# A hybrid SSD, Hyena and PEER block: one-hots of eight tokens in one comparison, 16-bit key lookup, expert activations kept in PSUM

## The chip, the cores and the metric

The kernel runs on one core of a Trainium2 chip. The metric is the time of one execution in microseconds (us) of device time: 4247.77 us before, the median of three runs (4242.83 to 4251.62). Engines: TensorE (PE, with PEld for its weight loads) multiplies matrices, VectorE (DVE), ScalarE (ACT) and GpSimd (POOL) work on elements, SyncE (SP) issues DMAs. SBUF is the on-chip memory, PSUM the small memory into which TensorE writes.

## The reference

One layer of a diffusion backbone over 1024 tokens of width 1024, with a context of 256. Two kinds of token mixing (a bidirectional Mamba-2 scan and a gated long convolution) come first, and the channel mixing after them, PEER, is the part that concerns us. Cut to it:

```python
def block(hb):                                    # 128 tokens
    q = (hb @ wq).reshape(128, 8, 2, 128)
    s = einsum('thsd,snd->thsn', q, subkeys)      # 8 heads, two key sets of 128
    s1, i1 = top_k(s[:, :, 0], 16)
    s2, i2 = top_k(s[:, :, 1], 16)
    sc, ci = top_k(all 256 sums s1 + s2, 16)
    e1 = i1 at ci // 16;  e2 = i2 at ci % 16
    idx = e1 * 128 + e2                           # one of 16384 experts
    gate = softmax(sc)
    act = gelu(hb . u_tab[idx]) * gate            # 8 x 16 experts per token
    return sum of act * v_tab[idx]
```

## The kernel before

Mixing and output projection take the first 1740 us or so and are not touched. Then eight blocks of 128 tokens are treated in two ways. For the last three blocks (`NB - ND`) the rows of the chosen experts are gathered from DRAM, one DMA of 128 rows at a time on GpSimd's queue, and VectorE multiplies them (class `Experts`, `gathered`). For the first five (`ND`, 640 tokens) every one of 128 groups of 128 experts is computed densely on TensorE, and a table of gates, mostly zeros, picks the chosen ones.

Routing. `firsts` multiplies tokens with the keys (`qacc`) and takes the 16 best per half with VectorE's max, index and replace instructions (`top16`); the 32-bit integer indices `r_ix` are cast to `r_idx`. `second` takes the 16 best of 112 candidate sums, splits their positions (`r_pos`, `r_pof`), and looks up the key index by a one-hot `r_oh` of 16 per choice, multiplied by the indices on GpSimd and summed on VectorE. `spread` builds the gate table of a block: for every token a one-hot of the first key times the gate (128 choices in the partitions, 128 keys in the row) and a one-hot of the second key, whose product on TensorE is the token's 128x128 table. It takes eight tokens at a time: the first one-hot (`e1`, named `r_e` in the trace, as is `e2`) of two tokens is made on ScalarE, of two on GpSimd and of four on VectorE, the second ones in one comparison on VectorE. A table goes to DRAM by `r_st`. GpSimd also makes the low parts of the keys (`wk_l`).

All products with 32-bit accuracy are made of a rounded high part and the rest (`split`: ScalarE copies to the high part, VectorE or GpSimd subtracts). `score` multiplies one expert group's `u` (parts `x_uh`, `x_ul`) with the 640 tokens in two halves of 320 (24 matmuls each, PSUM tile `x_s`, two banks) and applies Gelu. 48 groups (`NE`, `AHEAD`) are scored during the routing (`beside`) and stored in DRAM as `d_A`.

Expert stage (`run`). Groups go by four (`SC`). `up` loads or scores a group's activations `x_a`, multiplies them by the gates `x_g` and splits them to `x_ah`, `x_al`. `down` multiplies these with the group's value rows (`x_vh`, `x_vl`, made from `x_vr` by `load_v` on ScalarE and GpSimd) for one block and half of the columns, and VectorE adds the result `x_acc` to `x_o`. Between them `some` calls up the next gathered rows.

The order on each engine is not the order of the code: a scheduler places each instruction by a simulated time line within what data and buffers permit. Each engine works its list in that order; one that waits holds up all behind it on its engine.

Of the kernel before, what the change touches and what calls it, by code (L numbers as in the profile page):

```python
# [10 lines left out]
F32 = mybir.dt.float32  # L11
# [1268 lines left out]
E1A = 2  # L1280
RB = 4
E1P = 2
# [7 lines left out]
class Route:  # L1290
# [70 lines left out]
    def first(self, b, c, terms, wk, ps, bufs):  # L1361
# [9 lines left out]
        ix = wk.tile([128, 2, 16], U32, name="r_ix", bufs=2)  # L1371
        tmp = wk.tile([128, 128], F32, name="r_tmp", bufs=2)
        for j in range(2):
            self.top16(self.val[:, b, 2 * c + j], ix[:, j], sc[:, j], tmp)
        nc.vector.tensor_copy(self.idx[:, b, 2 * c:2 * c + 2], ix)
# [11 lines left out]
    def second(self, b, wk):  # L1387
# [4 lines left out]
        val, idf = self.val[:, b], self.idx[:, b]  # L1392
# [18 lines left out]
        V.tensor_copy(pof, pos)  # L1411
# [7 lines left out]
        for t in range(2):  # L1419
            oh = wk.tile([128, 8, 16, 16], F32, name="r_oh", bufs=1)  # L1420
# [3 lines left out]
            nc.gpsimd.tensor_mul(oh, oh, idf[:, t:16:2, None, :].to_broadcast([128, 8, 16, 16]))  # L1424
            yield
            if t < TRD:
                for n in (8, 4, 2, 1):
                    nc.gpsimd.tensor_add(oh[..., :n] if n > 1 else e[:, t, :, :, None], oh[..., :n], oh[..., n:2 * n])
            else:
                V.tensor_reduce(e[:, t].rearrange("p h k -> p (h k)"), ohv, axis=AX.X, op=ALU.add)  # L1430
# [13 lines left out]
    def spread(self, b, ef, g, wk, ps, pq):  # L1444
# [6 lines left out]
        T = wk.tile([128, 4, 128], F32, name="r_T", bufs=2)  # L1451
        nc.scalar.activation(T[:, :3], p[:, :3], AF.Copy)
        nc.scalar.activation(T[:, 3], p[:, 2], AF.Copy, scale=-1.0)
        for q in range(128 // GT):
            st = wk.tile([128, 128, GT], F32, name="r_st", bufs=2)
            for t8 in range(GT // 8):
                t0 = q * GT + t8 * 8
                e1 = wk.tile([128, 8, 128], F32, name="r_e1", bufs=3)
                for m in range(8):
                    t = t0 + m  # L1460
                    if m < E1A:
                        nc.scalar.activation(e1[:, m], self.iota, AF.Abs, scale=-1.0, bias=T[:, 0, t:t + 1])
                        nc.scalar.activation(e1[:, m], e1[:, m], AF.Relu, scale=T[:, 3, t:t + 1], bias=T[:, 2, t:t + 1])
                    elif m < E1A + E1P:
                        nc.gpsimd.tensor_scalar(e1[:, m], self.iota, T[:, 0, t:t + 1], T[:, 2, t:t + 1],
                                                op0=ALU.is_equal, op1=ALU.mult)
                    else:
                        V.scalar_tensor_tensor(e1[:, m], self.iota, T[:, 0, t:t + 1],
                                               T[:, 2, t:t + 1].to_broadcast([128, 128]), op0=ALU.is_equal, op1=ALU.mult)
                e2 = wk.tile([128, 8, 128], F32, name="r_e2", bufs=2)  # L1470
                (nc.gpsimd if t8 < E2P else V).tensor_tensor(e2, self.iota[:, None, :].to_broadcast([128, 8, 128]),
                                T[:, 1, t0:t0 + 8, None].to_broadcast([128, 8, 128]), op=ALU.is_equal)
# [10 lines left out]
class Experts:  # L1483
# [24 lines left out]
    def beside(self, x, tiles):  # L1508
# [3 lines left out]
        while self.n < min(int(self.ahead), NE):  # L1512
            self.K.nc.sync.dma_start(self.K.T["A"][self.n], self.score())
# [112 lines left out]
    def score(self):  # L1626
# [10 lines left out]
        a = wk.tile([128, TD], F32, name="x_a", bufs=XA)  # L1637
        for m in range(SN):
            ms = slice(m * SW, (m + 1) * SW)
            s = ps.tile([128, 512], F32, name="x_s", bufs=2)  # L1640
# [293 lines left out]
```

## Time and profile before

| | us |
|---|---|
| median of three runs | 4247.77 |
| profiled execution | 4236.63 |
| its span, first to last instruction | 4234.9 |
| busy: PE, DVE | 3766.8, 3434.8 |
| busy: ACT, POOL | 1373.3, 2218.0 |

The mean granted clock of TensorE is 0.947 of full speed. All rows below come from the profiled execution, which is 11 us shorter than the median. Busy time is that in which an engine had an instruction in work, which includes the time that an instruction stood still after it began. Where a group of instructions of one form shows a mean well over its median, some of them stood.

### The profile page before, as it was taken

How to read it: one execution, taken by the hardware profiler on the slowest of the kernel's cores; microseconds unless marked ns; L12 is line 12 of the kernel's file. 1: busy time of each engine (PE TensorE's matmuls, PEld its weight loads, DVE VectorE, ACT ScalarE, POOL GpSimd, SP SyncE). 2: the span in 40 equal slices, each digit the busy share in tenths (PEclk: the TensorE clock that was granted, in tenths of full speed). 3: DMA queues.
4: the chain of work that ended last, by engine and by line, in shares of the span. 5: the costliest groups of instructions: out<-in, count | busy, mean ns of one | idle time of the engine just before them, and what ended most of it. 6: DMA issues, size and time to landing. Idle time of an engine off the chain costs nothing. (4 is left out here: it accounts for less than half of the span.)

```text
span 4234.9 us, 59929 instructions
## 1 busy us (share of the span) xinstructions
PE 3766.8 (89%) x21481; PEld 3307.3 (78%) x21481; DVE 3434.8 (81%) x6389; ACT 1373.3 (32%) x2567; POOL 2218.0 (52%) x1723
## 2 busy tenths in 40 slices
PE   5999999898888887789998877899989999989995
PEld 4787887777877786688998876788878888878884
DVE  5665887556889795599999996798878888878998
ACT  3233333326454121232225665222222222222221
POOL 2232323244344221065737785676767677667675
PEclk9999999998898998899999999999999999999997
DMA  6333433467774546567645546899989999989997
GB/s 209 103 123 103 130 112 133 134 194 223 228 233 142 168 148 180 166 214 250 232 134 206 201 170 218 285 338 322 354 314 340 317 326 340 342 310 341 337 322 258
DMA packets 509674, 974.09 MB, mean 230 GB/s; under 512 B 33771, under 2 KB 291231, under 8 KB 506432
## 3 DMA queue, kind: packets, MB, share of 16 engines
q1 hardware_dynamic: 395616, 557.25, 40.2%
q0 software_dynamic: 110880, 405.98, 26.2%
q10 hardware_dynamic: 2880, 7.03, 0.5%
q8 instruction: 169, 2.77, 0.3%
q14 instruction: 129, 1.06, 0.1%
HBM read 823.20 MB, written 146.95 MB: 229 GB/s over the span
## 5 line engine op out<-in xcount | busy, mean ns | idle before, releaser
L1643 PE MATMUL x_s<-fTh,x_uh 128*128 128x320 f32 x2048 | 640.9, 313 | 12.1 <-ACT x_a L1644 11.9
L1643 PE MATMUL x_s<-fTh,x_ul 128*128 128x320 f32 x2048 | 638.9, 312 | 7.2 <-DVE x_ul L1604 7.2
L1643 PE MATMUL x_s<-fTl,x_uh 128*128 128x320 f32 x2048 | 640.0, 313 | 0.0
L1683 PE MATMUL x_acc<-x_vl,x_ah 128*128 128x512 f32 x1280 | 514.1, 402 | 15.1 <-POOL x_vl L1615 15.1
L1683 PE MATMUL x_acc<-x_vh,x_ah 128*128 128x512 f32 x1280 | 449.8, 404 | 82.7 <-ACT x_vh L1614 60.8
L1520 POOL DMA_INDIRECT rows<-in_peer_u_dram,ids x384 | 415.1, 1081 | 197.3 <-DVE rows L1544 65.1
L1557 DVE SCALAR_TENSOR_TENSOR e_p<-rows,e_a,e_p 128x1024 f32<-128x1024 f32 x381 | 489.8, 1286 | 30.6 <-DMA rows<-in_peer_v_dram,ids 19.2
L1683 PE MATMUL x_acc<-x_vh,x_al 128*128 128x512 f32 x1280 | 509.6, 399 | 0.0
L1544 DVE SCALAR_TENSOR_TENSOR rows<-rows,e_p 128x1024 f32<-128x1024 f32 x384 | 455.5, 1210 | 41.7 <-DMA rows<-in_peer_u_dram,ids 39.6
L1520 POOL DMA_INDIRECT rows<-in_peer_v_dram,ids x384 | 397.7, 1036 | 140.5 <-issue 64.0
L1615 POOL TENSOR_TENSOR x_vl<-x_vr,x_vh 128x512 fp32r<-128x512 f32 x256 | 340.8, 1335 | 190.1 <-ACT x_vh L1614 178.9
L1643 PEld LDWEIGHTS x_s<-fTh,x_uh 128*128 128x128 f32 x2048 | 389.3, 190 | 25.8 <-ACT x_a L1644 16.7
L1643 PEld LDWEIGHTS x_s<-fTh,x_ul 128*128 128x128 f32 x2048 | 389.0, 190 | 17.0 <-DVE x_ul L1604 8.3
L1643 PEld LDWEIGHTS x_s<-fTl,x_uh 128*128 128x128 f32 x2048 | 389.3, 190 | 9.2
L1683 PEld LDWEIGHTS x_acc<-x_vh,x_ah 128*128 128x128 f32 x1280 | 241.9, 193 | 135.5 <-ACT x_vh L1614 67.5
L1683 PEld LDWEIGHTS x_acc<-x_vl,x_ah 128*128 128x128 f32 x1280 | 247.7, 194 | 69.3 <-POOL x_vl L1615 23.5
L1614 ACT ACTIVATE x_vh<-x_vr 128x512 fp32r<-128x512 f32 x256 | 159.7, 627 | 421.8 <-DMA x_vr<-in_peer_v_dram 351.4
L1683 PEld LDWEIGHTS x_acc<-x_vh,x_al 128*128 128x128 f32 x1280 | 247.2, 193 | 48.9
L199 PE MATMUL mm<-xl,whi 128*128 128x512 f32 (+1 forms) x784 | 263.6, 410 | 8.2 <-DVE xl L51 8.2
L199 PE MATMUL mm<-xh,whi 128*128 128x512 f32 (+1 forms) x784 | 263.9, 412 | 7.4 <-DVE acc L235 3.6
L51 POOL TENSOR_TENSOR wlo<-wraw,whi 128x1024 fp32r<-128x1024 f32 (+1 forms) x49 | 121.1, 2473 | 280.9 <-ACT whi L50 260.3
L199 PE MATMUL mm<-xh,wlo 128*128 128x512 f32 (+1 forms) x784 | 263.3, 411 | 0.4 <-POOL wlo L51 0.4
(382 smaller groups left out, 8748.9 us busy)
## 6 DMA issues: line engine op xcount, KB each, us to landing
x_raw<-in_peer_uT_dram SPq DMA_DIRECT2D x128, 512.0 KB
x_vr<-in_peer_v_dram SPq DMA_DIRECT2D x256, 256.0 KB
d_G<-r_st SPq DMA_DIRECT2D x20, 2048.0 KB
x_g<-d_G SPq DMA_DIRECT2D x32, 1280.0 KB
wraw<-in_w_mod_dram SPq DMA_DIRECT2D x32, 1024.0 KB
wraw<-in_w_in_dram SPq DMA_DIRECT2D x24, 1024.0 KB
wk_w<-d_WK SPq DMA_DIRECT2D x24, 1024.0 KB
d_kr<-h_k SPq DMA_DIRECT2D x32, 512.0 KB
```

Source lines behind the costliest of these rows:

```text
L51: (self.nc.gpsimd if pool else self.nc.vector).tensor_sub(lo, src, hi.bitcast(F32))
L199: nc.tensor.matmul(p, w[:, k], x[j][:, k, t0:t0 + n], start=(k == 0 and q == 0), stop=(k == 7 and q == 2))
L1520: nc.gpsimd.indirect_dma_start(out=r, out_offset=None, in_=table, in_offset=bass.IndirectOffsetOnAxis(ap=ids[:, j:j + 1], axis=0))
L1544: nc.vector.scalar_tensor_tensor(r, r, 1.0, f, op0=ALU.mult, op1=ALU.mult, accum_out=d[:, j:j + 1])
L1557: nc.vector.scalar_tensor_tensor(acc, r, a[:, j:j + 1], acc, op0=ALU.mult, op1=ALU.add)
L1614: nc.scalar.activation(hi, raw, AF.Copy)
L1615: self.pace = nc.gpsimd.tensor_sub(lo, raw, hi.bitcast(F32)).ins
L1643: nc.tensor.matmul(s[:, :SW], w[:, k], x[:, k, ms], start=(k == 0 and q == 0), stop=(k == 7 and q == 2))
L1683: self.K.nc.tensor.matmul(p, a[x][:, bs], v[w], start=(m == 0 and q == 0), stop=(m == SC - 1 and q == 2))
```

## The change

Four edits, all after 1740 us.

- `top16` writes its indices straight into `r_idx`, now a 32-bit integer table; `second` casts a block's 256 indices at once to 16 bits (`r_if`) on ScalarE, as it does the positions.
- The key one-hot `r_oh` is made in 16 bits with two buffers; its product with the key indices moves from GpSimd to VectorE.
- In `spread`, one comparison on VectorE makes the first one-hots of eight tokens (`e0`). Three tokens (`GP`) are multiplied by the gate in one instruction on GpSimd, five on ScalarE, one copy each with the gate as scale. The negated gates are no longer needed.
- In the expert stage, Gelu writes back to PSUM; the gate product is made there in halves of 320, and both parts are taken from there. A loaded activation is multiplied from SBUF into a score bank, so that it takes both banks too.

```diff
-        self.idx = mid.tile([128, NB, 16, 16], F32, name="r_idx")
+        self.idx = mid.tile([128, NB, 16, 16], U32, name="r_idx")
...
-        nc.vector.tensor_copy(self.idx[:, b, 2 * c:2 * c + 2], ix)
...
-        val, idf = self.val[:, b], self.idx[:, b]
+        val = self.val[:, b]
+        idf = wk.tile([128, 16, 16], BF16, name="r_if", bufs=1)
+        nc.scalar.activation(idf, self.idx[:, b], AF.Copy)
...
-        V.tensor_copy(pof, pos)
+        nc.scalar.activation(pof, pos, AF.Copy)
...
-            oh = wk.tile([128, 8, 16, 16], F32, name="r_oh", bufs=1)
+            oh = wk.tile([128, 8, 16, 16], BF16, name="r_oh", bufs=2)
...
-            nc.gpsimd.tensor_mul(oh, oh, idf[:, t:16:2, None, :].to_broadcast([128, 8, 16, 16]))
+            V.tensor_mul(oh, oh, idf[:, t:16:2, None, :].to_broadcast([128, 8, 16, 16]))
...
-                    if m < E1A:
-                        nc.scalar.activation(e1[:, m], self.iota, AF.Abs, scale=-1.0, bias=T[:, 0, t:t + 1])
-                        nc.scalar.activation(e1[:, m], e1[:, m], AF.Relu, scale=T[:, 3, t:t + 1], bias=T[:, 2, t:t + 1])
-                    elif m < E1A + E1P:
-                        nc.gpsimd.tensor_scalar(e1[:, m], self.iota, T[:, 0, t:t + 1], T[:, 2, t:t + 1],
-                                                op0=ALU.is_equal, op1=ALU.mult)
-                    else:
-                        V.scalar_tensor_tensor(e1[:, m], self.iota, T[:, 0, t:t + 1],
-                                               T[:, 2, t:t + 1].to_broadcast([128, 128]), op0=ALU.is_equal, op1=ALU.mult)
...
+                e0 = wk.tile([128, 8, 128], F32, name="r_e0", bufs=2)
+                V.tensor_tensor(e0, io, T[:, 0, ts, None].to_broadcast([128, 8, 128]), op=ALU.is_equal)
...
+                nc.gpsimd.tensor_mul(e1[:, :GP], e0[:, :GP], T[:, 2, t0:t0 + GP, None].to_broadcast([128, GP, 128]))
+                for m in range(GP, 8):
+                    nc.scalar.activation(e1[:, m], e0[:, m], AF.Copy, scale=T[:, 2, t0 + m:t0 + m + 1])
...
-            nc.scalar.activation(a[:, ms], s[:, :SW], AF.Gelu)
-        return a
+            nc.scalar.activation(s if out is None else out[:, m * SW:(m + 1) * SW], s, AF.Gelu)
+            yield s
...
+            halves = ((a[:, n * SW:(n + 1) * SW], self.ps.tile([128, 512], F32, name="x_s", bufs=2)[:, :SW]) for n in range(SN))
         else:
-            a = self.score()
-        av = a.rearrange("p (q t) -> p q t", t=GT)
-        (nc.gpsimd if self.turn('m', MP) else nc.vector).tensor_mul(av, av, self.g4[:, :, m, :])
+            halves = ((s, s) for s in self.score())
...
-        K.split(a, hi, lo)
+        nq = SW // GT
+        for n, (x, s) in enumerate(halves):
+            nc.vector.tensor_mul(s.rearrange("p (q t) -> p q t", t=GT), x.rearrange("p (q t) -> p q t", t=GT),
+                                 self.g4[:, n * nq:(n + 1) * nq, m, :])
+            K.split(s, hi[:, n * SW:(n + 1) * SW], lo[:, n * SW:(n + 1) * SW])
```

The order on the engines shows three places. First VectorE in the gate tables of the first block: before, in each group of eight tokens four one-hots and one comparison, between other routing and gathered rows (`rows`).

```order
L1471 TENSOR_TENSOR r_e_18188<-iota_f,r_T 128x1024
L1468 SCALAR_TENSOR_TENSOR r_e_18275<-iota_f,r_T 128x128 x4
L1544 SCALAR_TENSOR_TENSOR rows,e_d<-rows,e_p 128x1024
L1345 MATCH_REPLACE r_tmp_19019<-r_s,r_cand 128x112
L1544 SCALAR_TENSOR_TENSOR rows,e_d<-rows,e_p 128x1024
L1471 TENSOR_TENSOR r_e_18286<-iota_f,r_T 128x1024
L1468 SCALAR_TENSOR_TENSOR r_e_18303<-iota_f,r_T 128x128 x4
```

After, the same place has two comparisons per group; lines are two or more lower in the changed file (L1454 makes `e0`, L1456 `e2`, L1535 is the gathered row).

```order
L1456 TENSOR_TENSOR r_e_18027<-iota_f,r_T 128x1024
L1535 SCALAR_TENSOR_TENSOR rows,e_d<-rows,e_p 128x1024
L1454 TENSOR_TENSOR r_e_18050<-iota_f,r_T 128x1024
L1345 MAX_INDEX r_ci<-r_s,r_tmp_17951 128x8
L1456 TENSOR_TENSOR r_e_18052<-iota_f,r_T 128x1024
L1454 TENSOR_TENSOR r_e_18146<-iota_f,r_T 128x1024
L1456 TENSOR_TENSOR r_e_18148<-iota_f,r_T 128x1024
```

Four one-hots became one comparison of eight tokens; nothing else changes in number here.

Second, VectorE in the expert stage, with the buffers' numbers. Before, a scored group (33084) is multiplied whole and subtracted whole; the subtractions of two loaded ones (x_al_32956, x_al_33032) stand ahead of it.

```order
L51 TENSOR_TENSOR x_al_32956<-x_a_32952,x_ah_32955 128x640
L1544 SCALAR_TENSOR_TENSOR rows_32570,e_d_31152<-rows_32570,e_p_31153 128x1024
L51 TENSOR_TENSOR x_al_33032<-x_a_33028,x_ah_33031 128x640
L1689 TENSOR_TENSOR x_o_22886<-x_o_22886,x_acc_32872 128x512
L1544 SCALAR_TENSOR_TENSOR rows_32637,e_d_31152<-rows_32637,e_p_31153 128x1024
L1660 TENSOR_TENSOR x_a_33084<-x_a_33084,x_g_32950 128x640
L1544 SCALAR_TENSOR_TENSOR rows_32640,e_d_31152<-rows_32640,e_p_31153 128x1024
L1544 SCALAR_TENSOR_TENSOR rows_32643,e_d_31152<-rows_32643,e_p_31153 128x1024
L51 TENSOR_TENSOR x_al_33139<-x_a_33084,x_ah_33138 128x640
```

After, the loaded group 33381: the product of its second half (bank 33386), gathered rows (L1535) and additions to the result (L1681), then the subtraction that frees its first bank (33382).

```order
L1653 TENSOR_TENSOR x_s_33386<-x_a_33378,x_g_33376 128x320
L1535 SCALAR_TENSOR_TENSOR rows_32927,e_d_31125<-rows_32927,e_p_31126 128x1024
L1535 SCALAR_TENSOR_TENSOR rows_32950,e_d_31125<-rows_32950,e_p_31126 128x1024
L1535 SCALAR_TENSOR_TENSOR rows_32967,e_d_31125<-rows_32967,e_p_31126 128x1024
L1535 SCALAR_TENSOR_TENSOR rows_32970,e_d_31125<-rows_32970,e_p_31126 128x1024
L1535 SCALAR_TENSOR_TENSOR rows_33001,e_d_31125<-rows_33001,e_p_31126 128x1024
L1681 TENSOR_TENSOR x_o_22609<-x_o_22609,x_acc_33068 128x512
L1535 SCALAR_TENSOR_TENSOR rows_33018,e_d_31125<-rows_33018,e_p_31126 128x1024
L1681 TENSOR_TENSOR x_o_22609<-x_o_22609,x_acc_33094 128x512
L1681 TENSOR_TENSOR x_o_22609<-x_o_22609,x_acc_33186 128x512
L1681 TENSOR_TENSOR x_o_22609<-x_o_22609,x_acc_33281 128x512
L51 TENSOR_TENSOR x_al_33381<-x_s_33382,x_ah_33380 128x320
```

The product now stands in a score bank while gathered rows pass, where it stood in SBUF before.

Third, ScalarE in the expert stage. Before, Gelu (L1644) takes a score out of its bank; the copy to the high part (L50) reads SBUF.

```order
L50 ACTIVATE x_ah_30469<-x_a_30466 128x640
L1644 ACTIVATE x_a_30519<-x_s_30520 128x320
L1644 ACTIVATE x_a_30519<-x_s_30546 128x320
L50 ACTIVATE x_ah_30573<-x_a_30519 128x640
L1614 ACTIVATE x_vh_30328<-x_vr_30326 128x512
L1644 ACTIVATE x_a_30612<-x_s_30613 128x320
L1614 ACTIVATE x_vh_30334<-x_vr_30332 128x512
```

After, L1633 is Gelu in place, L50 reads the bank, L1605 copies value rows; the loaded group's copies (33380) come behind four of value rows.

```order
L1633 ACTIVATE x_s_33243<-x_s_33243 128x320
L1605 ACTIVATE x_vh_33036<-x_vr_33034 128x512
L50 ACTIVATE x_ah_33206<-x_s_33243 128x320
L1605 ACTIVATE x_vh_33042<-x_vr_33040 128x512
L1605 ACTIVATE x_vh_33048<-x_vr_33046 128x512
L1605 ACTIVATE x_vh_33083<-x_vr_33081 128x512
L50 ACTIVATE x_ah_33380<-x_s_33382 128x320
L50 ACTIVATE x_ah_33380<-x_s_33386 128x320
L1605 ACTIVATE x_vh_33313<-x_vr_33311 128x512
L1605 ACTIVATE x_vh_33319<-x_vr_33317 128x512
L1633 ACTIVATE x_s_33470<-x_s_33470 128x320
L50 ACTIVATE x_ah_33462<-x_s_33470 128x320
```

So a bank's way to being free passes ScalarE twice and VectorE twice, where it passed ScalarE once.

## Rows read from the trace of the kernel before

**Rows 1.** Busy time of the engines by stage; start:end and length, us.
```profile
core 0: us, PE busy (x) PEld busy (x) DVE busy (x) ACT busy (x) POOL busy (x), PEclk, DMA share, GB/s
...
1740.00:2250.00 510.00, 450.44 (x3097) 434.70 (x3096) 484.47 (x1731) 144.47 (x233) 254.22 (x133) 0.96 0.57 197
...
2250.00:2590.00 340.00, 285.22 (x2085) 277.96 (x2083) 325.52 (x665) 230.73 (x534) 284.75 (x193) 0.94 0.51 194
...
2611.00:4189.00 1578.00, 1483.99 (x7632) 1297.83 (x7632) 1346.31 (x1564) 392.04 (x634) 1100.88 (x941) 0.97 0.92 326
```

**Rows 2.** Groups of the routing, 1740:2620; busy us, mean ns, idle before.
```profile
L1468 DVE SCALAR_TENSOR_TENSOR r_e<-iota_f,r_T 128x128 f32<-128x128 f32 x320 | 134.4, 478 | 0.0
...
L1375 DVE CAST r_idx<-r_ix 128x32 f32<-128x32 uint32 x62 | 48.6, 784 | 0.2
...
L1422 DVE TENSOR_TENSOR r_oh<-r_pof,iota_f 128x2048 f32<-128x2048 f32 x16 | 43.4, 2713 | 0.1
...
L1604 DVE TENSOR_TENSOR x_ul<-x_raw,x_uh 128x1024 fp32r<-128x1024 f32 x24 | 42.1, 1753 | 0.0
...
L1424 POOL TENSOR_TENSOR r_oh<-r_oh,r_idx 128x2048 f32<-128x2048 f32 x16 | 77.2, 4825 | 16.0 <-DVE r_oh L1422 15.9
...
L51 POOL TENSOR_TENSOR wk_l<-wk_w,wk_h 128x2048 fp32r<-128x2048 f32 x16 | 74.8, 4678 | 19.2 <-ACT wk_h L50 19.0
...
L1604 POOL TENSOR_TENSOR x_ul<-x_raw,x_uh 128x1024 fp32r<-128x1024 f32 x25 | 63.3, 2533 | 180.9 <-ACT x_uh L1603 180.5 <-DVE r_ci L1344 0.2
...
L1462 ACT ACTIVATE r_e<-iota_f,r_T 128x128 f32<-128x128 f32 x160 | 54.9, 396 | 0.0
...
L1463 ACT ACTIVATE r_e<-r_e,r_T 128x128 f32<-128x128 f32 x160 | 71.9, 486 | 0.0
```

**Rows 3.** The same tiles, 1740:2620: duration min/median/max in ns.
```profile
L1468 DVE SCALAR_TENSOR_TENSOR r_e<-iota_f,r_T x320: 336/341/5447, 2249.0 to 2586.4; 128x128 f32<-128x128 f32 x160
...
L1375 DVE CAST r_idx<-r_ix x62: 149/168/5443, 1740.6 to 2176.9; 128x32 f32<-128x32 uint32 x62
...
L1422 DVE TENSOR_TENSOR r_oh<-r_pof,iota_f x16: 2268/2279/6645, 1824.4 to 2506.5; 128x2048 f32<-128x2048 f32 x16
...
L1604 DVE TENSOR_TENSOR x_ul<-x_raw,x_uh x24: 1199/1214/5553, 1831.5 to 2498.8; 128x1024 fp32r<-128x1024 f32 x24
```

**Rows 4.** Timeline of VectorE and GpSimd about 2300; start us, us.
```profile
2298.30 3.30 DVE L1468 SCALAR_TENSOR_TENSOR r_e<-iota_f,r_T 128x128 f32<-128x128 f32 x4
...
2298.59 2.53 POOL L1604 TENSOR_TENSOR x_ul<-x_raw,x_uh 128x1024 fp32r<-128x1024 f32 x1 [3.30 <-ACT x_uh L1603]
...
2302.83 1.21 DVE L1471 TENSOR_TENSOR r_e<-iota_f,r_T 128x1024 f32<-128x1024 f32 x1
...
2303.96 1.14 DVE L1468 SCALAR_TENSOR_TENSOR r_e<-iota_f,r_T 128x128 f32<-128x128 f32 x4
```

**Rows 5.** Groups of the expert stage, 2620:4235, VectorE.
```profile
L1660 DVE TENSOR_TENSOR x_a<-x_a,x_g 128x640 f32<-128x640 f32 x125 | 160.4, 1289 | 86.5 <-DMA x_a<-d_A 47.8 <-ACT x_a L1644 36.2 <-ACT x_uh L1603 2.5
...
L51 DVE TENSOR_TENSOR x_al<-x_a,x_ah 128x640 fp32r<-128x640 f32 x125 | 141.9, 1143 | 4.0 <-ACT x_ah L50 2.8 <-issue 0.7 <-PE x_acc L1683 0.4
...
L1689 DVE TENSOR_TENSOR x_o<-x_o,x_acc 128x512 f32<-128x512 f32 x310 | 200.6, 680 | 36.8 <-PE x_acc L1683 30.5 <-PE x_s L1643 3.9 <-issue 1.9
```

**Rows 6.** Tile x_a, 2611:4189: duration min/median/max in ns.
```profile
L1660 DVE TENSOR_TENSOR x_a<-x_a,x_g x127: 809/822/4507, 2612.0 to 4156.9; 128x640 f32<-128x640 f32 x127
...
L51 DVE TENSOR_TENSOR x_al<-x_a,x_ah x128: 808/819/5847, 2612.8 to 4160.0; 128x640 fp32r<-128x640 f32 x128
```

**Rows 7.** Waits of the expert stage: us in total, times, longest.
```profile
ACT x_vh L1614 <- DMA x_vr<-in_peer_v_dram: 350.7, 95, 16.0
...
PE x_acc L1683 <- ACT x_vh L1614: 60.8, 18, 12.1
...
PE x_acc L1683 <- POOL x_vl L1615: 15.1, 16, 3.5
...
PE x_s L1643 <- ACT x_a L1644: 8.1, 5, 3.4
```

More of the change, by code (lines that the diff above doesn't have):

```diff
@@ L1279 @@
 SC = 4
-E1A = 2
 RB = 4
-E1P = 2
 XR = 2
@@ L1370, in first @@
         yield
-        ix = wk.tile([128, 2, 16], U32, name="r_ix", bufs=2)
         tmp = wk.tile([128, 128], F32, name="r_tmp", bufs=2)
         for j in range(2):
-            self.top16(self.val[:, b, 2 * c + j], ix[:, j], sc[:, j], tmp)
-        nc.vector.tensor_copy(self.idx[:, b, 2 * c:2 * c + 2], ix)
+            self.top16(self.val[:, b, 2 * c + j], self.idx[:, b, 2 * c + j], sc[:, j], tmp)
     def firsts(self, blocks, wk, ps):
@@ L1450, in spread @@
             nc.tensor.transpose(p[:, j], x, K.ident)
-        T = wk.tile([128, 4, 128], F32, name="r_T", bufs=2)
-        nc.scalar.activation(T[:, :3], p[:, :3], AF.Copy)
-        nc.scalar.activation(T[:, 3], p[:, 2], AF.Copy, scale=-1.0)
+        T = wk.tile([128, 3, 128], F32, name="r_T", bufs=2)
+        nc.scalar.activation(T, p[:, :3], AF.Copy)
         for q in range(128 // GT):
@@ L1512, in beside @@
         while self.n < min(int(self.ahead), NE):
-            self.K.nc.sync.dma_start(self.K.T["A"][self.n], self.score())
+            a = self.wk.tile([128, TD], F32, name="x_a", bufs=XA)
+            for _ in self.score(a):
+                pass
+            self.K.nc.sync.dma_start(self.K.T["A"][self.n], a)
             self.n += 1
@@ L1624, in gates, with score @@
         return t
-    def score(self):
+    def score(self, out=None):
         nc, wk, ps, R = self.K.nc, self.wk, self.ps, self.R
@@ L1636, in score @@
         uh, ul = self.parts.pop(0)
-        a = wk.tile([128, TD], F32, name="x_a", bufs=XA)
         for m in range(SN):
-            ms = slice(m * SW, (m + 1) * SW)
-            s = ps.tile([128, 512], F32, name="x_s", bufs=2)
+            s = ps.tile([128, 512], F32, name="x_s", bufs=2)[:, :SW]
             for k in range(8):
                 for q, (w, x) in enumerate(((uh, fh), (uh, fl), (ul, fh))):
-                    nc.tensor.matmul(s[:, :SW], w[:, k], x[:, k, ms], start=(k == 0 and q == 0), stop=(k == 7 and q == 2))
-            nc.scalar.activation(a[:, ms], s[:, :SW], AF.Gelu)
-        return a
+                    nc.tensor.matmul(s, w[:, k], x[:, k, m * SW:(m + 1) * SW], start=(k == 0 and q == 0), stop=(k == 7 and q == 2))
+            nc.scalar.activation(s if out is None else out[:, m * SW:(m + 1) * SW], s, AF.Gelu)
+            yield s
     def up(self, g, m):
@@ L1797 @@
 MP = 0
-E2P = 0
 KB = 2
@@ L1801 @@
 NE = 48
+GP = 3
 AHEAD = [4 * g + m for g in range(32) for m in range(2 - g % 2)]
@@ L1805 @@
 GB = 2
-TRD = 0
 VR = 2
```

17 lines of the change are left out of this document (6 added, 11 removed).

## The prediction, made before the run

> **What bounds the kernel now.** I read the busy time by stage first, because an average over 4234.9 us mixes stages with different limits [rows 1]. Nothing before about 1740 us is touched. From 1740 to 2250 (key scores, top-16) VectorE is busy 484 of 510 us, and from 2250 to 2590 (the gate tables) 326 of 340; TensorE has 450 and 285 there. So up to 2590 the length is the length of VectorE's queue, and a microsecond more or less on it counts nearly in full. From 2611 to 4189 (the expert stage) TensorE has 1484 of 1578 us, VectorE 1346, and the DMA engines 0.92: three resources near their end, TensorE first. The remaining 46 us are the ending, unchanged.
>
> Second, the groups of instructions of the routing, means beside medians [rows 2, 3]. A median far under the mean says that some instances stood still. The one-hot line of VectorE (L1468) has a median of 341 ns and a mean of 478; the key-index cast (L1375) 168 and 784, for 32 elements. The timeline shows the cause: while GpSimd's subtraction of 2.53 us runs, four one-hots take 3.30 us, and a few microseconds later 1.14 us [rows 4]. So VectorE's queue is part work and part standing behind GpSimd.
>
> Third, the expert stage: the gate multiplication takes 1289 ns in the mean and 822 in the median, the low-part subtraction 1143 and 819 [rows 5, 6], the same sign; the addition out of PSUM takes 680. TensorE's waits name the loaded value rows first (60.8 and 15.1 us) and the score banks with 8.1 us [rows 7].
>
> **Routing, VectorE's work.** The order shows that only these instructions of VectorE differ in number.
> - 320 one-hots with gate go: 1.14 us for four [rows 4], 0.28 each, makes -90 us.
> - 80 comparisons of eight tokens come. Their twin (L1471) gives way to the next instruction after 1.13 us (2302.83 to 2303.96 in [rows 4]): +90 us.
> - 64 index casts go, at the median less the 0.08 us in which neighbours overlap, 0.09 us: -6 us. The eight casts of positions go to ScalarE too; at worst each is as long as half a 1024-element comparison, so I book -3 us.
> - 16 multiplications of one-hots by key index come from GpSimd, now in 16 bits. The trace of before has no 16-bit operation on VectorE. The row of the same shape in 32 bits is 2279 ns [rows 3]: +35 us. If two elements went at a time it would be a 1024-element row, 1.13 us: +18 us. I take +35, by the row of the same shape.
>
> Together +26 us of work: eight tokens in one comparison cost what four one-hots and a half did.
>
> **Routing, standing behind GpSimd.** Mean less median, times the count [rows 2, 3]: one-hots 320 x 0.137 = 44 us, casts 62 x 0.616 = 38, low parts of u 24 x 0.54 = 13, key one-hots 16 x 0.43 = 7; 102 us in four groups. GpSimd's two-input operations that these stand behind sum to 77.2 + 74.8 + 63.3 = 215 us [rows 2]; so roughly half of their time is lost on VectorE. Afterwards the 77 us are gone, and 80 multiplications of 384 elements come, an estimate of 0.95 us each by the 1024-element row (2533 ns x 384/1024): 76 us. That is 214 us again. But the casts, which stood wherever GpSimd ran in the first stage, are no longer there to be caught; what still is (u parts, key one-hots) starts rarely. For the second stage nearly every operation of VectorE is one that can be caught, and the new multiplication becomes ready just as the next comparison runs. I take half of 76 for the new ones (38) and a quarter of 138 for the old (35): 73 us, a gain of 29. Bounds: all 76 and half of 138 lost, 145, which is 43 worse than now; or 20 for the new and 20 for the old, which is 62 better.
>
> The rule of the Trainium skill ("SBUF — State Buffer", section "Who interferes with whom") is that a VectorE instruction with two SBUF inputs and a GpSimd instruction that reads SBUF exclude each other for a whole instruction, and that one with a PSUM operand is free of it. [Rows 4, 6] agree for the first half. It speaks against the new GpSimd multiplication and for the PSUM form below; taken to the letter it is a rival below.
>
> **Routing, the other engines.** ScalarE's four operations per eight tokens (396 and 486 ns, twice each, 1.76 us) become five copies; between those two rows that is 2.0 to 2.4 us, 18 to 53 us more on 231 of 340 [rows 1, 2]. Hidden by VectorE's queue; without that cover it would be the 18 to 53 us. GpSimd is relieved. So the routing: +26 - 29 = -3 us, which I call nothing. Range from the bounds: -53 (18 for the 16-bit products, best standing) to +69.
>
> **Expert stage.** Per expert VectorE had one multiplication and one subtraction of 640 elements: 125 x (1.289 + 1.143) = 304 us [rows 5]. Now it has four of 320 with one operand in PSUM. By the 512-element row out of PSUM (680 ns) and some 1.02 ns per element (822 for 640, 1.21 us for 1024) one is 0.48 us, 500 of them 242 us. The 45 to 48 experts scored ahead still multiply from SBUF, so that part of the standing, 58 us x 48/128 = 22, stays. That frees 40 us by durations, and some 25 more as the short neighbours overlap more often: 40 to 65 of 1346 us. TensorE could give back at most its idle 94 us [rows 1]. VectorE is not what it waits for by name; it gains through ScalarE, which converts the value rows in the same queue as the activations, and through row buffers that come free earlier. I take a third of 60: -20 us. Bounds: +50 (first rival) and -60.
>
> What the change adds: a score bank is held until Gelu, product, copy and subtraction of its half are through. There are two banks, and the 48 loaded experts now take both as well. Ahead of the copy on ScalarE stand copies of value rows, between the product and the subtraction on VectorE gathered rows of 1.2 us (the length of the 1024-element rows); the next score on TensorE waits for all. The second and third pieces of order above show such a loaded expert, its copies after four value-row conversions.
>
> **Sum.** The profiled run took 4236.6 us (span 4234.9): -3 -20 makes about 4214. Its median over the runs shown is 4247.8, 11 more; I predict from that: about 4226 us.
>
> **Rivals.**
> 1. Score banks (slower). Of some 160 scored halves (80 experts) one in three finds its bank held 1 us too long: +50 us, against -10 from relieved VectorE and nothing in the routing: 4288. For it: ScalarE, which is now on the way to a free bank twice, stands 350.7 us before value rows that have not landed [rows 7], and two banks are few. Against it: now the score waits only 8.1 us for a bank [rows 7]. It decides from where the hold after Gelu is longer than the work that TensorE has between two halves in the same bank (the other half and a block of products).
> 2. The port (slower). Every GpSimd product of the tables shuts out a comparison for its full 0.95 us: 76 + 60 standing, routing +60, expert stage -20: 4288. The skill's page says so for each pair. For it: comparisons stand back to back. Against it: VectorE also has gathered rows and top-16 there, which are not caught.
> 3. More gain. The products of 16 bits go two at a time (-17), standing falls to 50 (-23 more), and the expert stage gives 35: about 4170. The Trainium skill ("VectorE: DVE Perf Modes", "The perf-mode tier table (the rule you actually need)") has 1224 ns for 2048 elements of 16 bits and 2293 in 32 bits; by it alone the sum would be some 16 us lower. No run shows it yet.
> 4. Nothing. VectorE's relief in the expert stage ends in the DMA, already at 0.92 [rows 1]: 4245.
>
> **How the numbers follow.** Forecast 0.48, rival 1 0.13, rival 2 0.11, rival 3 0.16, rival 4 0.12. This kernel tells no change within 0.2% (8.5 us). Of the forecast's 0.48, 0.42 is faster, 0.04 same, 0.02 slower; with rival 3 faster is 0.58; rival 4 gives 0.11 to the same, 0.15 in all; slower 0.27. The forecast's own range is 4200 to 4255; to hold 8 in 10 it reaches into the rivals, 4170 to 4285.
>
> **What would show it.** Up to about 2590 the end of the tables should move by less than 30 us; the comparison (L1454, L1456) should have a median of 1.2 us, its mean tells the standing (over 1.7 is rival 2); the 16-bit product 1.2 or 2.3 us. In the expert stage products and subtractions should be near 0.48 us with mean close to median. TensorE's wait for a score bank, now 8.1 us, above 50 us is rival 1. I am wrong if the tables end more than 50 us away, or if the expert stage grows.

## The result, and the profile after

The changed kernel takes 4308.05 us (median of 4 runs, 4301.98 to 4314.36), the kernel before 4249.69 us (median of 4, 4242.83 to 4253.48): ratio 1.0142, 95% interval 1.0125 to 1.0159. It is 1.4% slower; the forecast was 4226 us, and the time lies above the range of 4170 to 4285. The rows below are of the profiled executions, 4314.36 and 4236.63 us, which lie 78 us apart where the medians lie 58.

The busy time by stage, the same stretches as in [rows 1] (the program enters the routing 9 us later here: the first key-score matmul starts at 1725.2 us, before at 1715.9; over all runs of this document that start lies between 1711 and 1728):

```profile
core 0: us, PE busy (x) PEld busy (x) DVE busy (x) ACT busy (x) POOL busy (x), PEclk, DMA share, GB/s
1749.00:2213.00 464.00, 422.97 (x2963) 411.19 (x2961) 431.25 (x1589) 139.59 (x228) 203.57 (x118) 0.96 0.59 206
2213.00:2583.00 370.00, 305.54 (x2226) 293.57 (x2227) 363.97 (x513) 250.00 (x630) 177.77 (x112) 0.97 0.51 191
2601.00:4290.00 1689.00, 1516.57 (x7680) 1324.72 (x7680) 1293.64 (x1829) 412.01 (x771) 1063.22 (x955) 0.95 0.88 308
```

The last table matmul ends at 2583.4 us (before 2591.8), so from its own start the routing is 18 us shorter. The expert stage is 112 us longer, 1689 for 1577 us from the first to the last sum over value rows, and the ending is 22 us for 46, which gives back 24. In that stage VectorE is busy 53 us less, as forecast (71 less from the first sum to the end of the run, as the shorter ending put more of its work into the stage), but TensorE stands idle 172 us for 94, and its granted clock falls from 0.97 to 0.95 of 2.4 GHz, and it is busy 33 us longer, with one score of 48 matmuls more in the stretch. The DMA engines' share falls too, from 0.92 to 0.88: no engine is busy for a larger share of the stage, and all of them wait more.

In the routing, duration min/median/max in ns, answering to [rows 3]:

```profile
L1422 DVE TENSOR_TENSOR r_oh<-r_oh,r_if x16: 1201/1211/3921, 1842.7 to 2521.2; 128x2048 bf16<-128x2048 bf16 x16
...
L1454 DVE TENSOR_TENSOR r_e<-iota_f,r_T x80: 1168/1212/3402, 2202.9 to 2578.5; 128x1024 f32<-128x1024 f32 x80
L1456 DVE TENSOR_TENSOR r_e<-iota_f,r_T x80: 1199/1212/3407, 2205.9 to 2577.4; 128x1024 f32<-128x1024 f32 x80
L1458 POOL TENSOR_TENSOR r_e<-r_e,r_T x80: 820/1675/4486, 2212.6 to 2580.5; 128x384 f32<-128x384 f32 x80
```

and the groups with their means (busy us, mean ns, then the idle time before them):

```profile
L1464 PE MATMUL qg<-r_e,r_e 128*128 128x128 f32 x1280 | 173.3, 290 | 60.8 <-POOL r_e L1458 51.2 <-DVE r_e L1456 4.2 <-ACT r_e L1460 2.4
...
L1460 ACT ACTIVATE r_e<-r_e,r_T 128x128 f32<-128x128 f32 x400 | 125.9, 391 | 64.2 <-DVE r_e L1454 64.1
L1454 DVE TENSOR_TENSOR r_e<-iota_f,r_T 128x1024 f32<-128x1024 f32 x80 | 120.9, 1514 | 3.6 <-ACT r_T L1446 3.0 <-POOL r_e L1458 0.5
...
L1456 DVE TENSOR_TENSOR r_e<-iota_f,r_T 128x1024 f32<-128x1024 f32 x80 | 116.8, 1466 | 0.0
...
L1420 DVE TENSOR_TENSOR r_oh<-r_pof,iota_f 128x2048 bf16<-128x2048 f32 x16 | 45.7, 2895 | 0.0
...
L1595 DVE TENSOR_TENSOR x_ul<-x_raw,x_uh 128x1024 fp32r<-128x1024 f32 x24 | 35.7, 1489 | 0.5 <-ACT x_uh L1594 0.3 <-ACT r_st L1466 0.2
...
L1422 DVE TENSOR_TENSOR r_oh<-r_oh,r_if 128x2048 bf16<-128x2048 bf16 x16 | 23.0, 1459 | 0.0
```

The 16-bit product takes 1211 ns in the median for 2048 elements, about half of the 2279 ns of the 32-bit row of that shape. (The figure of the Trainium skill named in rival 3, "VectorE: DVE Perf Modes", 1224 ns, agrees.) The comparisons take 0.30 and 0.25 us more in the mean than in the median: they stand 44 us over 160. The key one-hots (2280 ns in the median), the low parts of u (1213) and the 16-bit product stand 10, 7 and 4 us: 65 in all, where it was 102 before.

In the expert stage, VectorE, answering to [rows 5] (same columns):

```profile
L51 DVE TENSOR_TENSOR x_al<-x_s,x_ah 128x320 fp32r<-128x320 f32 x256 | 121.0, 483 | 59.1 <-ACT x_ah L50 58.6
...
L1653 DVE TENSOR_TENSOR x_s<-x_s,x_g 128x320 f32<-128x320 f32 x160 | 79.1, 495 | 183.0 <-ACT x_s L1633 182.6
...
L1653 DVE TENSOR_TENSOR x_s<-x_a,x_g 128x320 f32<-128x320 f32 x95 | 66.5, 708 | 0.4
```

The durations are the ones forecast; the product of a loaded half is so in the median (492 ns), and its standing, 708 in the mean, was kept in the sum. The waits are not the ones forecast. TensorE's and ScalarE's, in us, times, longest, answering to [rows 7]:

```profile
PE x_acc L1675 <- ACT x_vh L1605: 121.0, 24, 10.6
PE x_acc L1675 <- POOL x_vl L1606: 21.6, 15, 5.0
...
PE x_s L1632 <- DVE x_al L51: 7.8, 7, 3.0
```

```profile
ACT x_vh L1605 <- DMA x_vr<-in_peer_v_dram: 321.8, 73, 14.1
ACT x_s L1633 <- PE x_s L1632: 304.2, 78, 8.7
ACT x_ah L50 <- DVE x_s L1653: 241.0, 171, 7.4
```

and the last two of these before:

```profile
ACT x_ah L50 <- DVE x_a L1660: 184.3, 67, 9.1
ACT x_a L1644 <- PE x_s L1643: 95.1, 36, 7.8
```

TensorE's wait for value rows (x_vh) is doubled, 121 us for 60.8. Its wait for a score bank, by which rival 1 was to be seen, is 7.8 us for 8.1. New is that ScalarE stands 304 us at a Gelu until TensorE has finished the score (before 95). A value row passes through that same queue. One such passage, from the timeline of the changed kernel (start us, us, and in brackets the idle time before it):

```profile
3169.70 0.44 ACT L50 ACTIVATE x_ah<-x_s 128x320 fp32r<-128x320 f32 x1 [1.20 <-DVE x_s L1653]
...
3176.54 1.06 ACT L1594 ACTIVATE x_uh<-x_raw 128x1024 fp32r<-128x1024 f32 x1 [3.97 <-PE x_s L1632]
...
3177.51 0.42 ACT L1633 ACTIVATE x_s<-x_s 128x320 f32<-128x320 f32 x1
...
3177.84 1.83 POOL L1511 DMA_INDIRECT rows<-in_peer_u_dram,ids  x1 [0.30 <-issue]
3177.86 0.61 ACT L1605 ACTIVATE x_vh<-x_vr 128x512 fp32r<-128x512 f32 x1
...
3179.69 1.28 POOL L1606 TENSOR_TENSOR x_vl<-x_vr,x_vh 128x512 fp32r<-128x512 f32 x1
...
3180.99 10.87 SPq L1602 DMA_DIRECT2D x_vr<-in_peer_v_dram  x1
```

The value row had landed at 3174.87 (last update of its load's semaphore). ScalarE stood at the copy of a u row until TensorE was through with a score, then did that copy and a Gelu, and took the value row 3.0 us late; GpSimd was issuing a gather until 3179.67 and subtracted 1.2 us late; and within 0.03 us of the subtraction's end the next load went into the buffer that came free. That is a loop: load, wait, copy, wait, subtract, issue. There are two buffers (VR = 2) and 256 value tiles, so the stage is 128 rounds of it. Its mean over the tiles, in us, worked out for each tile from the end of its issue, the last update of its semaphore that the trace holds (some are missing, so a load can be a little longer), its copy, its subtraction and the issue two tiles later (tiles 8 to 253):

```
                       load   wait for  copy   wait for  sub-    to next  round
                              ScalarE          GpSimd    tract   issue
before                 5.18   1.60      0.63   2.46      1.33    1.19     12.39
routing alone          5.30   1.50      0.63   2.47      1.33    1.26     12.49
halves in SBUF         5.48   1.54      0.63   2.33      1.33    1.49     12.80
loaded ones in SBUF    5.34   2.06      0.63   1.99      1.33    1.35     12.69
experts alone          5.17   1.95      0.63   2.25      1.31    1.74     13.05
changed kernel         5.20   2.41      0.63   2.02      1.32    1.65     13.21
```

128 x (13.21 - 12.39) = 105 of the 112 us. This says where the added time lies, not what bounds the stage: loads that run through the whole stage always make rounds that add up to it, with four buffers too (below). The load itself is the same. Of the 0.82 us, the wait for ScalarE adds 0.81, the wait for GpSimd gives back 0.44, and the step from the subtraction to the next issue adds 0.46. Of this last part 0.28 is that the issues on SP are longer (1.04 us for 0.76 in the mean); it does not pass through ScalarE, and no run takes it apart. For rows that had landed, what ScalarE did meanwhile sums to 394 us before and 595 after; standing at a Gelu for its score rose from 25 to 121 us of it, at a u copy for a score from 42 to 109, at an activation copy for its product from 35 to 85.

### The profile page after: what moved, and what is told of

Its sections match the earlier page's. It is cut to its first block, busy times and chain, and to the rows that moved or that the text cites. A ratio compares the mean times of both kernels' runs of the same rounds, so it can differ in the third digit from the quotient of the medians.

```text
span 4312.3 us, 59728 instructions
## 1 busy us (share of the span) xinstructions
PE 3788.9 (88%) x21481; PEld 3320.9 (77%) x21481; DVE 3354.1 (78%) x6349; ACT 1401.5 (33%) x2786; POOL 1997.3 (46%) x1627
## 3 DMA queue, kind: packets, MB, share of 16 engines
q14 instruction: 127, 1.04, 0.1%
## 5 line engine op out<-in xcount | busy, mean ns | idle before, releaser
L1632 PE MATMUL x_s<-fTh,x_uh 128*128 128x320 f32 x2048 | 645.5, 315 | 11.2 <-DVE x_al L51 7.8
L1675 PE MATMUL x_acc<-x_vh,x_ah 128*128 128x512 f32 x1280 | 458.6, 412 | 160.5 <-ACT x_vh L1605 121.0
L1511 POOL DMA_INDIRECT rows<-in_peer_u_dram,ids x384 | 394.5, 1027 | 189.7 <-DVE rows L1535 68.1
L1535 DVE SCALAR_TENSOR_TENSOR rows<-rows,e_p 128x1024 f32<-128x1024 f32 x384 | 459.0, 1209 | 27.8 <-DMA rows<-in_peer_u_dram,ids 27.4
L1511 POOL DMA_INDIRECT rows<-in_peer_v_dram,ids x384 | 370.3, 964 | 142.8 <-DVE e_p L1548 63.7
L1605 ACT ACTIVATE x_vh<-x_vr 128x512 fp32r<-128x512 f32 x256 | 159.2, 626 | 362.1 <-DMA x_vr<-in_peer_v_dram 329.8
L1681 DVE TENSOR_TENSOR x_o<-x_o,x_acc 128x512 f32<-128x512 f32 x310 | 201.5, 679 | 69.5 <-PE x_acc L1675 69.1
```

The source lines that it names most:

```text
L1511: nc.gpsimd.indirect_dma_start(out=r, out_offset=None, in_=table, in_offset=bass.IndirectOffsetOnAxis(ap=ids[:, j:j + 1], axis=0))
L1535: nc.vector.scalar_tensor_tensor(r, r, 1.0, f, op0=ALU.mult, op1=ALU.mult, accum_out=d[:, j:j + 1])
L1605: nc.scalar.activation(hi, raw, AF.Copy)
L1632: nc.tensor.matmul(s, w[:, k], x[:, k, m * SW:(m + 1) * SW], start=(k == 0 and q == 0), stop=(k == 7 and q == 2))
L1675: self.K.nc.tensor.matmul(p, a[x][:, bs], v[w], start=(m == 0 and q == 0), stop=(m == SC - 1 and q == 2))
L1681: self.K.nc.vector.tensor_add(dst, dst, p)
```

## Experiments: which part

Throughout, a diff is against the changed kernel unless it says otherwise. The first expectation names the four theories, BANKS, QUEUE, HALVES and ROUTING. First the two parts alone: `score`, `up` and `beside` of the kernel before in the changed kernel (routing alone), and those of the changed kernel in the one before (experts alone; the same lines the other way round, on the kernel before).

```
-            halves = ((s, s) for s in self.score())       # in up
+            a = self.score()
...
-            nc.vector.tensor_mul(s..., x..., self.g4[:, n * nq:(n + 1) * nq, m, :])
-            K.split(s, hi[:, n * SW:(n + 1) * SW], lo[:, n * SW:(n + 1) * SW])
+        (nc.gpsimd if self.turn('m', MP) else nc.vector).tensor_mul(av, av, self.g4[:, :, m, :])
+        K.split(a, hi, lo)
```

> The routing part of the change alone; scores, products and splits of the experts as before. Theories for the 112 us that the expert stage lost (1577 to 1689 us): BANKS (a score bank is held from the first score matmul to the last subtraction, and a loaded expert takes two banks too, so scores and loaded experts are worked out later), QUEUE (ScalarE does its work in order, and a Gelu or a copy that waits for VectorE's product of a half stands ahead of the copies of V rows), HALVES (twice as many short instructions, wherever they lie) and ROUTING (the routing part leaves something behind that slows the stage: another order, other transfers). BANKS, QUEUE and HALVES: the stage is as before, the routing 18 us shorter, so 4232 us. ROUTING: the stage stays near 1689 us, the time near 4300 us.

> The expert part of the change alone; the routing as before. BANKS, QUEUE and HALVES: the stage takes 1680 to 1695 us and the time is 4308 + 18 = 4326 us. ROUTING: the stage is as before, 1577 us, and the time 4250 us or a little less.

Measured: routing alone 4237.13 us (ratio to before 0.9970, 0.9951 to 0.9989), its stage 1587 us; experts alone 4304.67 us (1.0137, 1.0096 to 1.0178), its stage 1669 us. The loss is the expert part's; ROUTING falls. Experts alone is 21 us below the 4326 that the other three expected, and its stage 11 us below the least that they gave.

Then the two things that the expert part does, apart: loaded experts back in SBUF, and halves without PSUM.

```
-            halves = ((a[:, n * SW:(n + 1) * SW], self.ps.tile(..., name="x_s", bufs=2)[:, :SW]) for n in range(SN))
+            nc.vector.tensor_mul(av, av, self.g4[:, :, m, :])     # whole, in SBUF
+            K.split(a, hi, lo)
```

> The changed kernel, but the 48 experts whose activations come back from memory go the way of before: product in place in SBUF over 640 columns, one copy and one subtraction. The 80 scored ones stay in PSUM in halves. BANKS: the loaded experts no longer take the banks that the scores want, so most of the 112 us goes: 4215 to 4250 us. QUEUE and HALVES: only 48 of 128 experts change, so some 112 x 48/128 = 42 us: about 4265 us. ROUTING: no change, 4308 us.

```
-            halves = ((s, s) for s in self.score())
+            halves = (a[:, n * SW:(n + 1) * SW] for n, _ in enumerate(self.score(a)))   # product and split from a
```

> The changed kernel, but halves in SBUF: the Gelu writes to SBUF and frees the bank, loaded experts take no bank, and product, copy and subtraction still go half by half. BANKS: the loss goes, 4232 us or less. HALVES: the loss stays, 4300 us (the two products of a half read SBUF on both sides, so rather more). QUEUE: between the two, 4260 to 4300 us, since the copies still wait for a product of a half each, but the Gelu does not wait for a bank. ROUTING: 4308 us.

Measured: loaded experts in SBUF 4244.98 us (0.9993, 0.9976 to 1.0009), stage 1616; halves in SBUF 4265.41 us (1.0040, 1.0020 to 1.0060), stage 1624. Taking 48 of 128 experts out of PSUM gives back 63 of the 71 us between routing alone and the changed kernel, as BANKS said (QUEUE and HALVES allowed 42). It isn't the standing at a Gelu by itself: with loaded experts in SBUF ScalarE stands there as long as in the changed kernel (304 us), and a landed row still waits 2.06 us for ScalarE.

```profile
ACT x_s L1633 <- PE x_s L1632: 315.3, 85, 11.3
```

With halves in SBUF BANKS expected 4232 us or less and HALVES 4300; the 4265 lie in the range of QUEUE, 4260 to 4300. So the two runs do not single out one theory. Beside routing alone, halves in SBUF cost 28 us of their own, and the table shows that it isn't by the wait for ScalarE (1.54 us, as before). VectorE's rows of that run show more work:

```profile
L1654 DVE TENSOR_TENSOR x_a<-x_a,x_g 128x320 f32<-128x320 f32 x254 | 200.1, 809 | 94.3 <-DMA x_a<-d_A 63.9 <-ACT x_a L1633 30.5
...
L51 DVE TENSOR_TENSOR x_al<-x_a,x_ah 128x320 fp32r<-128x320 f32 x256 | 188.2, 762 | 9.1 <-ACT x_ah L50 8.7
```

In SBUF the half takes 809 and 762 ns in the mean, so two halves take 1618 and 1524 where the whole took 1289 and 1143 [rows 5]; that this makes the 28 us is argued, not shown. Out of PSUM a half of the same width takes 495 and 483. The port rule of the Trainium skill named in the prediction ("SBUF — State Buffer", "Who interferes with whom") agrees: what it exempts, an input in PSUM, is what stands least here, and the product of a loaded half, with both inputs in SBUF and its result in PSUM, stands (708).

## Experiments: banks

A third score bank, paid for with one of the four banks for sums, with that payment alone as its control, and the third bank given to loaded experts only:

```
-PA = 4
+PA = 3                                # c_pa3
-            s = ps.tile([128, 512], F32, name="x_s", bufs=2)[:, :SW]
+            s = ps.tile([128, 512], F32, name="x_s", bufs=self.sb)[:, :SW]   # e5: 3 in this stage, both places
-   ... self.ps.tile([128, 512], F32, name="x_s", bufs=2)[:, :SW]) for n
+   ... self.ps.tile([128, 512], F32, name="x_t", bufs=1)[:, :SW]) for n      # e8: loaded experts
```

> The changed kernel with three banks instead of four for the sums over V rows (PA = 3): the control of the next two, which need a bank. By the lines of the changed kernel TensorE waits 17 us for VectorE's addition of such a bank; with one bank fewer it is more. Estimate 4320 to 4350 us. No theory says more on it.

> The control with three score banks, shared by scores and loaded experts as before. BANKS (now in this form: a bank is held past the Gelu until the last subtraction, and loaded experts take their turn in it, so that the scores are worked out later, 35 us ahead of their use in place of 48): the scores are worked out early again and the time falls 40 to 70 us below the control. QUEUE and HALVES: as the control, within 10 us.

> The control with the third bank given to the loaded experts alone; the two others serve only the scores. BANKS: the scores no longer wait for a loaded expert's gates and copies: 40 to 63 us below the control, as the kernel with loaded experts in SBUF was 63 us below the changed one. QUEUE and HALVES: as the control or slower, since every copy is still there, and a loaded half now waits for the one before.

Measured: control 4325.53 (1.0193, 1.0165 to 1.0220), three shared 4289.94 (1.0083, 1.0053 to 1.0114), own bank 4300.57 us (1.0120, 1.0100 to 1.0140). 36 and 25 us below the control: the direction of BANKS, but each under the 40 that it gave as the least, and more than the 10 that QUEUE and HALVES allowed the first; neither expectation holds. By the names of the tiles, the activations of scored experts were ready 48 us (median) ahead of their first use before, 35 in the changed kernel, 33 in the control and 37 with three banks; 49 with halves in SBUF. In PSUM the scores come later, and a third bank mends that little (37 us ahead, where it was 48).

## Experiments: the value rows' loop

More buffers for value rows need 2 KB of a partition each, so a row buffer of the gathers (4 KB) is given up for them. A square of both, for the changed kernel and for routing alone:

```
-VR = 2
+VR = 3        # e6, e7; 4 in e11, e12
-RB2 = 7
+RB2 = 6       # c_rb6 and c_routing_rb6: this line alone
```

> The changed kernel with three buffers for the V rows that wait to be split (two before), paid for with one row buffer of the gathers (six for seven). QUEUE (V rows are copied late because ScalarE stands at a Gelu or a copy of another chain, their buffer comes free late and the next load starts late): the load runs through that, TensorE's 118 us for x_vh fall to 60 or less and the time to 4265 us or less. BANKS and HALVES: no change, 4290 to 4310 us, since the scores come as late as before.

> The routing part alone, with three buffers of V rows and six row buffers, as the run of the changed kernel with them (4232 us). QUEUE: the expert part costs only through the two V buffers; with three the two kernels are within 15 us of each other, 4217 to 4247 us. BANKS or HALVES as a cost of their own: the expert part still loses 40 us or more, so this one is at 4190 us or below.

> The changed kernel with six row buffers and still two of V rows: the control of the run with three. QUEUE: no gain from it, 4300 to 4325 us. If fewer gathers in flight were what helped there, it is near 4232 us.

> The routing part alone with six row buffers and two V buffers. QUEUE: the expert part's loss is that of the V buffers, so with two of them it stays: this one is 50 us or more below the changed kernel with six row buffers (4279 us), at 4210 to 4230 us. If the row buffer is what took the loss away, this one is within 25 us of it: 4255 us or more.

> The routing part alone with four V buffers and six row buffers. QUEUE: with three buffers the V rows had waited 5.8 us each after landing, so they are no longer the bound; the gathers are, whose last rows are added some 80 us after the last V sum there. So no further gain: 4200 to 4215 us.

> The changed kernel with four V buffers and six row buffers. QUEUE: as with three, 4220 to 4235 us, and within 20 us of the routing part alone with four. BANKS as a cost of its own: the scores are then the bound (with three V buffers 20 of 124 experts were ready under 5 us ahead of their use), and the loss stays at 20 us or more.

Measured, in us (expert stage in brackets):

```
value-row / row buffers   2 / 7            2 / 6            3 / 6            4 / 6
routing alone             4237.13 (1587)   4283.93 (1594)   4210.49 (1481)   4200.50 (1467)
changed kernel            4308.05 (1689)   4279.04 (1595)   4232.49 (1507)   4179.74 (1461)
```

The third buffer takes 47 us off the changed kernel beside its control, the fourth 53 more; off routing alone they take 73 and 10. With three, TensorE's wait for x_vh is 33.6 us (121 in the changed kernel, 70.1 with six row buffers alone), and the expert part still costs 22 us, where QUEUE allowed 15 and BANKS asked 40. With four it gains 21 us, more than any theory gave it; both expected 4220 us or more. That this is VectorE's relief, left over once the loop has buffers enough, is not shown: of the 22 us between these two profiled executions 10 lie ahead of the first value sum, 6 in the stage and 7 in the ending. The changed kernel with four is the best version of all, 0.9846 of the kernel before (0.9820 to 0.9872). Its stage and TensorE's waits:

```profile
2598.00:4059.00 1461.00, 1448.90 (x7680) 1285.34 (x7680) 1224.97 (x1767) 408.12 (x761) 996.52 (x895) 1.00 0.95 333
```

```profile
PE x_acc L1675 <- ACT x_ah L50: 20.4, 2, 17.7
PE x_s L1632 <- DVE x_al L51: 4.1, 5, 1.3
PE x_acc L1675 <- POOL x_vl L1606: 3.0, 3, 1.4
PE x_acc L1675 <- ACT x_vh L1605: 1.4, 1, 1.4
```

TensorE waits 1.4 us for x_vh in place of 121 and works 1449 of 1461 us, and its granted clock is 1.00 of 2.4 GHz, where it was 0.95 with 172 us of idle time. Worked out as above, a round is now 22.94 us, in which a landed row waits 11.23 us for ScalarE; 64 such rounds are the stage again. What is late next is the gathers: 54 of their 384 second rows are added after the last value sum (before: 2), and 118 us lie behind it. The Trainium skill ("Trainium Kernel Development and Optimization", "Best Practices") advises to double-buffer loads; here two buffers were a bound and two more were worth 99 us beside their control, so the advice is a least, not an end.

Two more of the expectations of QUEUE failed. Six row buffers alone were to change nothing, and took 29 us off the changed kernel; and routing alone with six was to be 50 us better than that, and was 5 us worse. The other reading on record there, that the row buffer is what took the loss away, asked for 4255 us or more, and 4283.93 is that. With six, 29 and 35 gathered rows are left for the ending, which grows to 85 and 93 us (from 22 and 46); the loop's round is 12.50 and 12.53 us, the same for both kernels. So the loss of the expert part needs, beside two value buffers, the seventh row in flight. In which queue that row does it isn't settled: without it, in the changed kernel, the wait for GpSimd falls from 2.02 to 1.52 us, that for ScalarE from 2.41 to 2.10. Nor does the effect of the expert part along the square, 71 and -5 and 22 and -21 us, follow from any of the theories.

That the loss might belong to one chance order, since each kernel's instructions are put in order anew, was tried by moving at most 4 of the 768 gathers (the 931 in the first expectation below is not their number):

```
-LASTG = -8
+LASTG = -12     # o1, and o3 on routing alone; -4 in o2
```

> The changed kernel with its gathers spread a little otherwise (LASTG = -12 for -8), which moves at most 4 gathers of 931 and some 6 us of work but gives another order. QUEUE as a cost of the expert part (PSUM held, ScalarE late for the V rows): 4290 to 4325 us as before. ORDER (the loss is that of one order, better or worse by chance): anywhere from 4240 to 4310 us, and 30 us or more from the changed kernel or from the next.

> The same with LASTG = -4. QUEUE: 4290 to 4325 us. ORDER: as for the one before, and not the same time as it.

> The routing part alone with LASTG = -12. QUEUE: 4225 to 4250 us, as with -8 (4237 us). ORDER: anywhere from 4220 to 4290 us.

Measured: 4302.59 (1.0130, 1.0097 to 1.0163) and 4295.64 us (1.0117, 1.0081 to 1.0153); routing alone 4219.65 us (0.9933, 0.9915 to 0.9950), 5 us under what QUEUE allowed. Over the orders the changed kernel is at 4296 to 4308 and routing alone at 4220 to 4237, with rounds of 13.1 to 13.2 and 12.5 us. The loss belongs to the expert part; an order is worth some 15 us. Of the three smaller effects in the square, -5, 22 and -21 us, none is far outside that, and no other order was tried there.

Two more runs. One takes the copy out of ScalarE's queue altogether:

```
-        nc.scalar.activation(hi, raw, AF.Copy)
+        nc.gpsimd.tensor_copy(hi, raw)          # in load_v
```

> The changed kernel, but the upper part of a V row is copied by GpSimd, which also takes the difference, and not by ScalarE. In the changed kernel a V row that has landed waits 2.4 us on average for ScalarE and then 2.0 us for GpSimd; a cycle of one of the two V buffers is 13.2 us, and 128 of them are the stage. QUEUE: the first wait goes, the copy takes 0.6 to 1.3 us there as the subtraction does, GpSimd is busy 150 to 330 us more of its 1066 of 1707; a cycle comes to 11.5 to 12.8 us and the time to 4200 to 4265 us. BANKS and HALVES: ScalarE's order is no matter, 4300 us or more.

Measured: 4411.72 us (1.0379, 1.0343 to 1.0415), a plain miss (4200 to 4265 us expected). A row of GpSimd shows where the wait went:

```profile
L1605 POOL CAST x_vh<-x_vr 128x512 fp32r<-128x512 f32 x254 | 164.7, 651 | 368.9 <-DMA x_vr<-in_peer_v_dram 329.1 <-PE x_acc L1675 38.6 <-PE x_s L1632 0.2
```

The copy is as quick as on ScalarE, but GpSimd now stands 329 us at value rows that have not landed, with gathers queued behind, where before ScalarE stood. The row still waits 2.40 us after landing and the subtraction another 3.00, more than half of the one and nearly half of the other behind the issuing of gathers: a round of 14.03. This points to the place in an in-order queue as the cost, whichever engine's; that GpSimd also has 165 us more to do was not separated from it.

The other, thought best before the square was known, keeps scored experts in PSUM and loads the others in halves of 320 through three small buffers, with all seven row buffers:

```
+            for n in range(SN):                            # in up, where e is in AHEAD
+                a = wk.tile([128, SW], F32, name="x_b", bufs=3)
+                nc.sync.dma_start(a, K.T["A"][AHEAD.index(e)][:, n * SW:(n + 1) * SW])
...
-VR = 2
+VR = 3
```

> Scored experts in PSUM, loaded ones in SBUF, but loaded and worked on in halves of 320 columns through three small buffers, which frees 1.25 KB of a partition and so pays for a third V buffer with all seven row buffers. QUEUE: the V rows no longer set the pace; next are the gathers and the DMA engines (0.92 of the stage before): 4180 to 4225 us, below both kernels. BANKS: 4235 us. HALVES: 4255 us.

Measured: 4224.47 us (0.9936, 0.9918 to 0.9954), as QUEUE said, at the upper end, and 11 us below what BANKS said, which is less than an order is worth; four buffers in the changed kernel are 45 us better.

## Why the prediction was wrong

- Routing: -3 forecast, -18 measured, and 13 to 18 in every run with the routing part. The 16-bit product was mis-sized (35 taken, 18 was the bound): 17 us. Standing was nearly right: 65 us for the 73 forecast, of which 44 at the comparisons, where 38 were taken for the new product on GpSimd. These two would make -28; the other 10 us are put down to no row. Not foreseen were TensorE's 51.2 us for the GpSimd product, whose median is 1.68 us for the 0.95 estimated. ScalarE's five copies are 1.96 us, just under the 2.0 to 2.4.
- Expert stage, durations: right. Products and subtractions 0.48 to 0.50 us (0.71 in the mean where a loaded half comes from SBUF), VectorE 53 us less busy (40 to 65 forecast).
- Expert stage, the price: this is the step that failed. "It gains through ScalarE, which converts the value rows in the same queue as the activations" was booked as -20; measured are +112 in the stage, +88 with the shorter ending. The sum priced VectorE's relief, took the value rows' wait of [rows 7] as given, and put the longer hold of a score bank, by loaded experts too, at nothing: it stood only in rival 1. The runs show 63 of the 71 us that the expert part costs come with the loaded experts' products in score banks. The added time lies in the round of the value rows through ScalarE, GpSimd and SP with two buffers, 13.21 for 12.39 us: more waiting, not more work. With four value-row buffers, or with two and a row buffer of the gathers less, the loss is gone. What in that loop turns the seventh row buffer into the loss stays open, and so does whether it is the bank or the loaded halves' place in ScalarE's queue that costs. That four buffers give -21 us, the forecast's -20, is luck as far as the runs show.
- Rival 1 had the direction and part of the cause, a bank held longer (a third bank gives back 25 to 36 us), but a wrong place for it: TensorE's wait for a bank stayed at 7.8 us and the price showed at x_vh. Its 50 us were half of the stage's loss. That the delayed score holds up value rows behind its Gelu and its u copy was not in the text.
- Rivals 2 and 4 are out: the means stay under 1.7 us, and the DMA engines got less busy, not more. Of rival 3 the 16-bit product came true; standing did not fall to 50 us, and the expert stage did not give 35.

## What to carry to other kernels

Before pricing an edit by busy time, write down the round of each buffer that a waiting engine names: load, waits, work, release. The length of the round times tiles over buffers doesn't tell whether it is the bound, as it comes to the stage's length in any case (128 x 13.21 us with two buffers, 64 x 22.94 with four). What a landed tile waits tells more: 2.4 us for ScalarE with two buffers, 11.2 with four. An in-order engine hands a wait on to everything queued behind it, so a new wait can show up at another chain's name: here at the value rows, not at the score bank. Adding a buffer to that round is the test, and can turn a losing edit into a gain; what pays for the buffer needs a control of its own, as here the control alone took 29 of 76 us.

## What the runs showed of the hardware

- GpSimd copied a 512-element row from 32 bits to the rounded form in 0.65 us, ScalarE in 0.63, but GpSimd's subtraction of the same size took 1.31.
- An issue on SP can itself be held: the load at 3180.99 took 10.87 us to issue, right after the gates' load of 1280 KB, where the median is 0.33; issues over 2 us are 24 of 256 in the changed kernel and 19 before. Why it is held was not tried.
